# First and last norm of a hybrid trunk: a weight cast moved back, a turned tile order, paired stores

## The chip, the cores and the metric

The kernel runs on one core of one Trainium2 chip. Its time is the device time of one execution in microseconds (us), and a kernel is given by the median of several runs. Five engines work side by side, each through its own queue in order: TensorE (PE in the profile, with its weight loads as PEld), VectorE (DVE), ScalarE (ACT), GpSimd (POOL) and SyncE (SP), which issues transfers. ScalarE has a queue for transfers as well (ACTq).

## The reference

One layer of a hybrid trunk on x of 2048 tokens by 1024 features, all in float32:

```python
def rmsnorm(x, w):
    y = xf * lax.rsqrt(jnp.mean(xf * xf, axis=-1, keepdims=True) + EPS)
    return (y * w.astype(jnp.float32)).astype(x.dtype)

h = rmsnorm(x, norm_mix_w)
proj = jnp.einsum("btd,dc->btc", h, w_in)
u_b, u_c, u_h, z, xbc, dt_raw = jnp.split(proj, SPLITS, axis=-1)
y_a = short_conv_mixer(u_b, u_c, u_h, short_conv_w)
y_b = ssd_mixer(z, xbc, dt_raw, ...)
x = x + jnp.einsum("btc,cd->btd", concatenate([y_a, y_b]), w_out)
h = rmsnorm(x, norm_mlp_w)
hid = jnp.square(jax.nn.relu(jnp.einsum("btd,df->btf", h, w_up)))
x = x + jnp.einsum("btf,fd->btd", hid, w_down)
return rmsnorm(x, final_norm_w)
```

The change touches the first line (the norm ahead of the input projection, for the first 512 tokens) and the last two (the end of the down projection and the final norm, for the second 1024 tokens).

## The kernel before, in words

Features lie on the 128 partitions and tokens along the free axis: x is eight tiles of 128 features, in blocks of 512 tokens. A float32 product is made of three matmuls: each operand is split into a high part, cast by ScalarE (`whi` for weights, `uh` for data), and a low part, which VectorE subtracts (`wlo`, `ul`); the products high-high, high-low and low-high are added in PSUM. Most of the kernel multiplies by a scheme of seven products in place of eight, which is not touched here.

**The start** (`first_block`, L476 to L578). TensorE first runs 36 matmuls on a constant, `warm(on, 36)`, which nobody reads. SyncE issues, in this order: the first token rows (`tokens`), the first quarter of x, the table `cv` with norm weights and other constants (62 KB: 124 floats, 496 bytes, on each partition), three weight tiles of 512 KB (`load_w`, columns 24, 25, 26 of the input projection), and the rest of x. ScalarE squares the token rows and adds them up; square root and reciprocal give one factor for each token, with the token on the partition. To bring these factors to the free axis, VectorE multiplies the identity by them (`diag`) and TensorE multiplies ones by `diag` into the PSUM bank `prb`: each row of `prb` then holds the factors of the tokens. This is the spread. It is done in two halves of 256 columns.

Then a list written out by hand sets the order of ScalarE and VectorE. The helper `line` (its function `on`, L466 in the profile) puts each instruction behind the one before on its engine. `scale(k)` multiplies block k of x by norm weight and `prb` on VectorE and casts it on ScalarE (in two halves for k = 0), and for k above 3 it also squares a row of the next tokens on ScalarE. `lower(k)` makes the low part `ul` on VectorE. `high(i, j)` casts half j (four of the eight feature blocks) of weight tile i on ScalarE, `low(i, j)` makes its low part on VectorE. TensorE's order is fixed too, in `group`: for the first block of x it runs the high-high product of column tile 0, then its low weight, then column tile 1, then column tile 2, then the low weight of tile 1; the low weight of tile 2 comes in the next block. `low(0, 0)` stands behind `scale(0)`, and `high(0, 1)` behind `high(0, 0)`.

**The tail** (`rest`, L1196 to L1249, and `norm_out`, L1251 to L1272). After the last chain of seven products, three quarters of the down projection's outputs of the second 1024 tokens miss some terms: column pair d = 1 three blocks of features, d = 2 two, d = 3 one (`REST`, L1330). They are added by plain products, for 512 tokens first and then for two times 256. Each pair gives two tiles, d and d + 4; a tile takes 18, 12 or 6 matmuls (`mm3`) in a half of 256 tokens. VectorE adds each to what is there (L1240, the eviction), ScalarE squares it (L1217), VectorE adds the square to a running sum (L1219), except for the last tiles, whose squares are held apart. `reduce` (L129, L133 in the profile) sums over the features by matmuls with one column of ones into `pst`; `root` takes the square root on ScalarE (L149), the reciprocal on VectorE (L150) and builds the diagonal (L152); `spread` (L176) runs the spread into `prb` (L178) and copies it to SBUF on ScalarE (L181). VectorE then multiplies tiles by norm weight and `prb` (L1266). GpSimd's tiles (`slow`) don't read `prb`: they are multiplied by the norm weight on ScalarE beforehand (L1257) and by the copy on GpSimd (L1264). Each of the eight tiles is stored by a transfer of its own (L1270), in the last half four by SyncE and four by ScalarE's queue. A norm's steps are a generator: `step()` runs the next piece between the tiles of the next column block, and the framework's scheduler then sets the order on each engine.

Of the kernel before, what the change touches and what calls it, by code (L numbers as in the profile page):

```python
# [16 lines left out]
P = 128  # L17
# [22 lines left out]
def trunk(ctx: ExitStack, tc: tile.TileContext, x, x_tok, w_in, w_dt, w_out, w_up, w_down, cvec, hrow, out):  # L40
# [30 lines left out]
    cv = const.tile([P, NCV + 4], F32, name="cv")  # L71
    ident = const.tile([P, P], F32, name="ident")
# [9 lines left out]
    eps = cv[:, NCV : NCV + 1]  # L82
    nc.vector.memset(eps, EPS)
    nc.scalar.activation(cv[:, NCV + 1 : NCV + 2], eps, AF.Sqrt)
# [38 lines left out]
    class Rstd:  # L123
# [5 lines left out]
        def reduce(self, *accs):  # L129
            pst = psum("tp", "pst", 2)  # L130
            for i, acc in enumerate(accs):
                for c in range(self.n):
                    nc.tensor.matmul(  # L133
                        pst[:, c : c + 1],
                        acc[:, c * P : (c + 1) * P],
                        ones[:, 0:1],
                        start=(i + c == 0),
                        stop=(i == len(accs) - 1),
                        skip_group_check=True,
                    )  # L140
            self.sums = pst[:, 0 : self.n]
# [34 lines left out]
        def spread(self, rb=None):  # L176
            prb = self.ps = psum("tp", "prb", 2)[:, 0 : self.w]
            nc.tensor.matmul(prb, ones, self.diag, start=True, stop=True)  # L178
            if rb is None:
                rb = self.pool.tile([P, TB], F32, tag="rstd", name="rstd", bufs=1)[:, 0 : self.w]  # L180
            nc.scalar.copy(rb, prb)  # L181
            return rb
# [229 lines left out]
    class Proj(Seven):  # L412
# [63 lines left out]
        def first_block(self, fs):  # L476
# [4 lines left out]
            self.warm(on, 36)  # L481
# [3 lines left out]
            nc.sync.dma_start(cv[:, 0:NCV], cvec)  # L485
# [17 lines left out]
            more = cv[:, NCV + 2 : NCV + 3]  # L503
# [9 lines left out]
            high(0, 1)  # L513
            diag = self.tmp("diag")
            prb = psum("tp", "prb", 2)
            for j in range(2):
                cs = slice(2 * j, 2 * j + 2)
                on(
                    nc.vector.tensor_tensor,
                    out=three(diag)[:, cs],  # L520
                    in0=ident.unsqueeze(1).to_broadcast([P, 2, P]),
                    in1=rs[:, cs].unsqueeze(2).to_broadcast([P, 2, P]),
                    op=ALU.mult,
                )
                on(nc.tensor.matmul, prb[:, half(j)], ones, diag[:, half(j)], start=True, stop=True)
# [31 lines left out]
            high(2, 0)  # L557
            low(0, 0)
            lower(0)
            scale(1)  # L560
            low(1, 0)
            low(2, 0)
            scale(2)
            lower(1)
            scale(3)
# [388 lines left out]
    class Mlp(Seven):  # L954
# [241 lines left out]
        def rest(self, ws):  # L1196
# [12 lines left out]
            for bb, t0, w in ((0, 0, TB), (1, 0, TB // 2), (1, TB // 2, TB // 2)):  # L1209
# [15 lines left out]
                for (d, fs, blocks), (whi, wlo) in ws:  # L1225
                    for i in range(2):
# [3 lines left out]
                        for _ in range(1 + final if d < 3 else 1 - final):  # L1230
                            step()
# [9 lines left out]
                        alone = (d, i) in (((2, 1), (3, 0), (3, 1)) if final else ((3, 1),))  # L1241
# [9 lines left out]
        def norm_out(self, tiles, bb, ts, st, final, *sums):  # L1251
            if not final:
                st.reduce(*sums)
            st.root()
            slow = (1, 4, 5)
# [3 lines left out]
            r = st.spread()  # L1259
            yield  # L1260
            for k in range(KD):
                o = tiles[k, bb][:, ts]
                if k in slow:
                    nc.gpsimd.tensor_tensor(out=o, in0=o, in1=r, op=ALU.mult)  # L1264
                else:
                    nc.vector.scalar_tensor_tensor(  # L1266
                        out=o, in0=o, scalar=col(C_NFIN, k), in1=st.ps, op0=ALU.mult, op1=ALU.mult
                    )
                queue = nc.scalar if final and k in (1, 3, 4, 5) else nc.sync
                queue.dma_start(out[NBB + bb, :, k, ts], o)  # L1270
# [59 lines left out]
    REST = [(1, [13, 14, 15]), (2, [14, 15]), (3, [15])]  # L1330
# [459 lines left out]
def _lay_out(inputs):  # L1790
# [17 lines left out]
            vec(np.repeat(f("d_skip")[0], 64)),  # L1808
        ],
# [36 lines left out]
```

## Time and profile before

| | us |
|---|---|
| median of 3 runs | 2612.67 |
| lowest, highest | 2609.78, 2613.57 |
| the profiled execution | 2614.04 |
| its span, first to last instruction | 2612.0 |

The profile is of one execution. In the lines of a timeline, the first figure is the start in us from the span's start, the second the duration in us (of several instructions together where xN stands at the end), then engine, line, operation, output<-input, shape; in brackets stands the idle time of the engine before it and what ended that. A line of TensorE gives matmuls; ends are modelled, so that a matmul's row reaches beyond the start of the next.

### The profile page before, as it was taken

To read this page: it belongs to the slowest core of one execution; us is meant where nothing else is said; L and a number is where in the kernel's file an instruction comes from. 1 tells how busy PE (TensorE), PEld (TensorE's weight loads), DVE (VectorE), ACT (ScalarE), POOL (GpSimd) and SP (SyncE) were. 2 spreads that over 40 slices of the span, in tenths; PEclk is the share of its full clock that TensorE was granted. 3 is DMA by queue.
4 is the path that set the end of the run, shared out by engine and by line. 5 is a ranking of instruction groups with operands and counts; after the bars stand their busy time and mean duration, and the time that the engine had idled before them with its cause. 6 is when DMAs were issued, how large, how long until landed. Compare 5 with 4: busy or idle time off the path is not lost.

```text
span 2612.0 us, 33558 instructions
## 1 busy us (share of the span) xinstructions
PE 2591.7 (99%) x12067; PEld 2134.1 (82%) x12067; DVE 1936.9 (74%) x2673; ACT 1433.9 (55%) x2185; POOL 59.0 (2%) x98
## 2 busy tenths in 40 slices
PE   9999999999999999999999999999999999999998
PEld 7888888788888888888888888888888888888887
DVE  7888666677778777877767765755558877888985
ACT  7553345876667676766336555655556444444443
POOL 0000000000000000000000000000000000000001
PEclk9999999999999999999999999999999999999999
DMA  5557445555555488876665674744447644665762
GB/s 213 206 200 256 181 145 183 179 159 170 182 163 170 139 276 277 276 227 209 206 213 206 233 270 142 252 159 145 160 144 271 199 149 150 215 207 179 242 206 77
DMA packets 284375, 511.52 MB, mean 196 GB/s; under 512 B 25264, under 2 KB 140976, under 8 KB 284208
## 3 DMA queue, kind: packets, MB, share of 16 engines
q1 hardware_dynamic: 283632, 508.86, 58.2%
q8 instruction: 94, 1.54, 0.2%
q14 instruction: 73, 0.60, 0.1%
q10 hardware_dynamic: 576, 0.52, 0.1%
HBM read 345.19 MB, written 164.10 MB: 195 GB/s over the span
## 4 chain that ended last, share of the span: by engine, by line
PE 65%; issue 25%; DMA 4%; DVE 3%; ACT 2%; SPq 0%; POOL 0%; POOLq 0%; DVEq 0%; ACTq 0%
PE px L271 10%; PE px L273 9%; PE px L272 9%; PE py L271 5%; PE py L272 5%; PE py L273 5%; PE pm L114 3%; PE pm L116 3%; PE pm L115 3%; PE pw L271 2%; PE pw L272 2%; PE pw L273 2%; DMA dec<-rd_d 2%; PE pm L466 1%; PE yd L1466 1%
## 5 line engine op out<-in xcount | busy, mean ns | idle before, releaser
L271 PE MATMUL px<-uh,whi 128*128 128x512 f32 x1672 | 655.4, 392 | 3.5 <-DVE acc L1157 2.2
L272 PE MATMUL px<-ul,whi 128*128 128x512 f32 x1672 | 651.0, 389 | 0.0
L273 PE MATMUL px<-uh,wlo 128*128 128x512 f32 x1672 | 651.0, 389 | 0.0
L271 PEld LDWEIGHTS px<-uh,whi 128*128 128x128 f32 x1672 | 313.9, 188 | 75.0 <-DVE acc L1157 5.9
L106 DVE TENSOR_TENSOR wlo<-wraw,whi 128x1024 fp32r<-128x1024 f32 (+2 forms) x224 | 226.7, 1012 | 193.3 <-ACT whi L105 193.1
L273 PEld LDWEIGHTS px<-uh,wlo 128*128 128x128 f32 x1672 | 313.9, 188 | 66.0 <-issue 0.2
L272 PEld LDWEIGHTS px<-ul,whi 128*128 128x128 f32 x1672 | 314.0, 188 | 63.7
L105 ACT CAST whi<-wraw 128x1024 fp32r<-128x1024 f32 (+2 forms) x224 | 197.9, 883 | 272.6 <-PE px L272 188.7
L105 ACT CAST whi<-s 128x1024 fp32r<-128x1024 f32 (+1 forms) x206 | 215.3, 1045 | 231.2 <-PE py L272 97.7
L271 PE MATMUL py<-uh,whi 128*128 128x512 f32 x836 | 326.7, 391 | 0.0
L272 PE MATMUL py<-ul,whi 128*128 128x512 f32 x836 | 325.4, 389 | 0.0
L273 PE MATMUL py<-uh,wlo 128*128 128x512 f32 x836 | 325.4, 389 | 0.0
L106 DVE TENSOR_TENSOR wlo<-s,whi 128x1024 fp32r<-128x1024 f32 (+1 forms) x206 | 250.4, 1216 | 76.8 <-ACT whi L105 75.5
L114 PE MATMUL pm<-uh,whi 128*128 128x512 f32 (+1 forms) x584 | 226.6, 388 | 0.0
L116 PE MATMUL pm<-uh,wlo 128*128 128x512 f32 (+1 forms) x584 | 223.2, 382 | 0.0
L115 PE MATMUL pm<-ul,whi 128*128 128x512 f32 (+1 forms) x584 | 222.9, 382 | 0.0
L271 PEld LDWEIGHTS py<-uh,whi 128*128 128x128 f32 x836 | 157.0, 188 | 32.9 <-issue 0.5
L273 PEld LDWEIGHTS py<-uh,wlo 128*128 128x128 f32 x836 | 157.0, 188 | 32.8
L272 PEld LDWEIGHTS py<-ul,whi 128*128 128x128 f32 x836 | 157.0, 188 | 32.2
L325 ACT CAST uh<-rh 128x1024 fp32r<-128x1024 f32 (+1 forms) x128 | 120.2, 944 | 98.0 <-PE py L273 61.7
L271 PE MATMUL pw<-uh,whi 128*128 128x512 f32 x418 | 163.2, 391 | 0.0
L273 PE MATMUL pw<-uh,wlo 128*128 128x512 f32 x418 | 162.8, 390 | 0.0
(250 smaller groups left out, 3840.3 us busy)
## 6 DMA issues: line engine op xcount, KB each, us to landing
hid_d<-e SPq DMA_DIRECT2D x96, 512.0 KB, 4.3
rh<-hid_d SPq DMA_DIRECT2D x96, 512.0 KB, 4.5
wraw<-w_in SPq DMA_DIRECT2D x67, 512.0 KB, 4.0
wraw<-w_up SPq DMA_DIRECT2D x62, 512.0 KB, 4.3
wraw<-w_down SPq DMA_DIRECT2D x100, 256.0 KB, 3.8
dec<-rd_d SPq DMA_DIRECT2D x32, 512.0 KB, 5.3
wraw<-w_out SPq DMA_DIRECT2D x32, 512.0 KB, 5.0
x_d<-xt SPq DMA_DIRECT2D x64, 256.0 KB, 3.6
```

Of the source, the lines that this page charges most:

```text
L105: nc.scalar.copy(hi, raw)
L106: eng.tensor_tensor(out=lo, in0=raw, in1=hi.bitcast(F32), op=ALU.subtract)
L114: nc.tensor.matmul(out, whi, hi, start=(k == 0), stop=False)
L115: nc.tensor.matmul(out, whi, lo, start=False, stop=False)
L116: nc.tensor.matmul(out, wlo, hi, start=False, stop=(k == nk - 1))
L271: nc.tensor.matmul(p, hi, h[0], start=bool(first and k == 0), stop=False, **kw)
L272: nc.tensor.matmul(p, hi, h[1], start=False, stop=False, **kw)
L273: nc.tensor.matmul(p, lo, h[0], start=False, stop=(k == len(g) - 1), **kw)
L325: nc.scalar.copy(p[i][0], t)
L466: last[engine] = make(*args, **kw).ins
L1466: nc.tensor.matmul(yd[(i % 2) * 64 : (i % 2) * 64 + 64, (i // 2) * L : (i // 2 + 1) * L], byhead(t["xdt"])[:, i, :], t["dec"][:, i, :], st ...
```

## The change

At the start: the table `cv` gets four columns of zeros on the host and is loaded as rows of 512 bytes; the constants that stood in its last columns move to a tile `small`. One warm-up matmul fewer. The diagonal is built by one instruction and spread by one matmul of 512 columns. `high(0, 1)` moves from behind `high(0, 0)` to behind `lower(1)`; `high(2, 0)` moves from ahead of `low(0, 0)` to behind `scale(1)`.

In the tail: `REST` runs d = 3, 2, 1, so the small tiles come first. In the last half two squares are held apart, not three. Behind the last sum matmul four matmuls of 512 columns on a constant run in a bank of their own. The last half's spread is run twice, into two banks: VectorE reads one, ScalarE copies the other. In the last half GpSimd multiplies two tiles (2 and 3) and VectorE six; before it were three and five; in the other blocks GpSimd's three are 2, 3 and 6 in place of 1, 4 and 5. In the last half tiles are multiplied into pair buffers, in the order 0, 1, 4, 5, 2, 3, 6, 7, and stored two at a time: pairs (0, 1) and (6, 7) by SyncE, (4, 5) and (2, 3) by ScalarE's queue.

```diff
+    small = const.tile([P, 4], F32, name="small")
-    eps = cv[:, NCV : NCV + 1]
+    eps = small[:, 0:1]
-    nc.scalar.activation(cv[:, NCV + 1 : NCV + 2], eps, AF.Sqrt)
+    nc.scalar.activation(small[:, 1:2], eps, AF.Sqrt)
...
-            self.sums = pst[:, 0 : self.n]
+            self.sums, self.reduced = pst[:, 0 : self.n], mm.ins
...
-        def spread(self, rb=None):
+        def spread(self, rb=None, apart=False):
             prb = self.ps = psum("tp", "prb", 2)[:, 0 : self.w]
             nc.tensor.matmul(prb, ones, self.diag, start=True, stop=True)
+            if apart:
+                prb = psum("mw", "prb")[:, 0 : self.w]
+                nc.tensor.matmul(prb, ones, self.diag, start=True, stop=True)
...
-            self.warm(on, 36)
+            self.warm(on, 35)
-            nc.sync.dma_start(cv[:, 0:NCV], cvec)
+            nc.sync.dma_start(cv, cvec)
-            more = cv[:, NCV + 2 : NCV + 3]
+            more = small[:, 2:3]
...
             high(0, 0)
-            high(0, 1)
             diag = self.tmp("diag")
             prb = psum("tp", "prb", 2)
-            for j in range(2):
-                cs = slice(2 * j, 2 * j + 2)
-                on(
-                    nc.vector.tensor_tensor,
-                    out=three(diag)[:, cs],
-                    in0=ident.unsqueeze(1).to_broadcast([P, 2, P]),
-                    in1=rs[:, cs].unsqueeze(2).to_broadcast([P, 2, P]),
-                    op=ALU.mult,
-                )
-                on(nc.tensor.matmul, prb[:, half(j)], ones, diag[:, half(j)], start=True, stop=True)
+            on(
+                nc.vector.tensor_tensor,
+                out=three(diag),
+                in0=ident.unsqueeze(1).to_broadcast([P, NC, P]),
+                in1=rs.unsqueeze(2).to_broadcast([P, NC, P]),
+                op=ALU.mult,
+            )
+            on(nc.tensor.matmul, prb, ones, diag, start=True, stop=True)
...
             scale(0)
             high(1, 0)
-            high(2, 0)
             low(0, 0)
             lower(0)
             scale(1)
+            high(2, 0)
             low(1, 0)
             low(2, 0)
             scale(2)
             lower(1)
+            high(0, 1)
             scale(3)
...
-                        for _ in range(1 + final if d < 3 else 1 - final):
+                        for _ in range(1 + final if d > 1 else 1 - final):
                             step()
-                        alone = (d, i) in (((2, 1), (3, 0), (3, 1)) if final else ((3, 1),))
+                        alone = d == 1 and i >= 1 - final
...
             if not final:
                 st.reduce(*sums)
+            else:
+                p = psum("mw", "pw")
+                with behind(st.reduced):
+                    for _ in range(4):
+                        nc.tensor.matmul(
+                            p, ones_r, ones_r.unsqueeze(1).to_broadcast([P, 4, P]), start=True, stop=True
+                        )
             st.root()
-            slow = (1, 4, 5)
+            slow = (2, 3) if final else (2, 3, 6)
...
-            r = st.spread()
+            r = st.spread(apart=final)
             yield
-            for k in range(KD):
-                o = tiles[k, bb][:, ts]
+            pair = None
+            for k in (0, 1, 4, 5, 2, 3, 6, 7) if final else range(KD):
+                o = to = tiles[k, bb][:, ts]
+                if final:
+                    if k % 2 == 0:
+                        pair = self.raw("fo")[:, :, 0 : st.w]
+                    to = pair[:, k % 2]
                 if k in slow:
-                    nc.gpsimd.tensor_tensor(out=o, in0=o, in1=r, op=ALU.mult)
+                    nc.gpsimd.tensor_tensor(out=to, in0=o, in1=r, op=ALU.mult)
                 else:
                     nc.vector.scalar_tensor_tensor(
-                        out=o, in0=o, scalar=col(C_NFIN, k), in1=st.ps, op0=ALU.mult, op1=ALU.mult
+                        out=to, in0=o, scalar=col(C_NFIN, k), in1=st.ps, op0=ALU.mult, op1=ALU.mult
                     )
-                queue = nc.scalar if final and k in (1, 3, 4, 5) else nc.sync
-                queue.dma_start(out[NBB + bb, :, k, ts], o)
+                if not final:
+                    nc.sync.dma_start(out[NBB + bb, :, k, ts], o)
+                elif k % 2:
+                    queue = nc.scalar if k in (3, 5) else nc.sync
+                    queue.dma_start(out[NBB + bb, :, k - 1 : k + 1, ts], pair)
...
-    REST = [(1, [13, 14, 15]), (2, [14, 15]), (3, [15])]
+    REST = [(3, [15]), (2, [14, 15]), (1, [13, 14, 15])]
...
+            np.zeros((P, 4), np.float32),
```

More of the change, by code (lines that the diff above doesn't have):

```diff
@@ L132, in reduce @@
                 for c in range(self.n):
-                    nc.tensor.matmul(
+                    mm = nc.tensor.matmul(
                         pst[:, c : c + 1],
```

## The prediction

> **What bounds the kernel now.** I read the page first, then the timeline of each engine over the first 33 us and the last 30 us, since the diff touches nothing between, and last the waits and the DMA landings of those stretches.
>
> ```profile
> PE 2591.7 (99%) x12067; PEld 2134.1 (82%) x12067; DVE 1936.9 (74%) x2673; ACT 1433.9 (55%) x2185; POOL 59.0 (2%) x98
> ```
>
> TensorE (PE) is busy for 99% of the span, so the end moves only with what TensorE waits for at the start, with what stands in its queue, and with the tail after its last matmul. The two changed places are of that kind. At the start, first TensorE, then ScalarE (ACT):
>
> ```profile
> 11.29 1.02 PE L466 MATMUL prb<-diag,ones_r 128*128 128x256 f32 x4
> ...
> 14.28 0.50 PE L466 MATMUL pm<-uh,whi 128*128 128x512 f32 x1 [1.27 <-ACT uh L466]
> ...
> 15.72 0.50 PE L466 MATMUL pm<-uh,whi 128*128 128x512 f32 x1
> ...
> 24.86 0.96 PE L466 MATMUL pm<-ul,whi 128*128 128x512 f32 x3 [0.33 <-DVE ul L466]
> ```
>
> ```profile
> 12.48 1.14 ACT L466 CAST whi<-wraw 128x512 fp32r<-128x512 f32 x2 [2.39 <-DMA wraw<-w_in]
> 13.52 0.71 ACT L466 CAST uh<-x 128x256 fp32r<-128x256 f32 x2
> 14.13 0.62 ACT L466 CAST whi<-wraw 128x512 fp32r<-128x512 f32 x1
> 15.04 0.62 ACT L466 CAST whi<-wraw 128x512 fp32r<-128x512 f32 x1 [0.29 <-DMA wraw<-w_in]
> 15.64 0.62 ACT L466 CAST uh<-x 128x512 fp32r<-128x512 f32 x1
> ```
>
> The first real matmul starts at 14.28, after 1.27 us without work, released by the cast `uh` on ScalarE. Ahead of that cast stand two weight casts (12.48, two in 1.14 us), and the first of them waited 2.39 us for the first weight to land. So the landing of the weight at about 12.45, then 0.52 us for each cast ahead, then 0.71 us for the two `uh` halves set 14.28. VectorE (DVE) in the same stretch:
>
> ```profile
> 10.40 0.76 DVE L466 TENSOR_TENSOR diag<-ident,rs 128x256 f32<-128x256 f32 x2
> 12.35 0.87 DVE L466 SCALAR_TENSOR_TENSOR x<-x,cv,prb 128x256 f32<-128x256 f32 x2 [1.19 <-PE prb L466]
> 13.14 0.68 DVE L466 TENSOR_TENSOR wlo<-wraw,whi 128x512 fp32r<-128x512 f32 x1
> 14.26 0.69 DVE L466 TENSOR_TENSOR ul<-x,uh 128x512 fp32r<-128x512 f32 x1 [0.43 <-ACT uh L466]
> 14.87 0.74 DVE L466 SCALAR_TENSOR_TENSOR x<-x,cv,prb 128x512 f32<-128x512 f32 x1
> 15.53 1.28 DVE L466 TENSOR_TENSOR wlo<-wraw,whi 128x512 fp32r<-128x512 f32 x2
> ```
>
> In these rows VectorE has one gap, 0.43 us for `uh`. It makes all low parts, and the last wait of TensorE in its rows is at 24.86, for VectorE's `ul` of the fifth block. So this start is bound first by ScalarE and then by VectorE's queue: a gain at 14.28 counts only if it is still there at 24.86.
>
> The tail, TensorE, ScalarE, VectorE, GpSimd (POOL), then DMA issues with KB and median us to landing:
>
> ```profile
> 2596.09 0.60 PE L178 MATMUL prb<-diag,ones_r 128*128 128x256 f32 x2
> ...
> 2601.19 0.28 PE L116 MATMUL pm<-uh,wlo 128*128 128x256 f32 x1
> 2601.31 0.50 PE L133 MATMUL pst<-ones_r,facc 128*128 128x1 f32 x4
> 2601.95 1.50 PE L133 MATMUL pst<-ones_r,sq 128*128 128x1 f32 x12
> 2604.46 0.70 PE L178 MATMUL prb<-diag,ones_r 128*128 128x256 f32 x2 [1.01 <-DVE diag L152]
> ```
>
> ```profile
> 2596.78 0.38 ACT L181 COPY rstd<-prb 128x256 f32<-128x256 f32 x1 [0.28 <-PE prb L178]
> ...
> 2601.48 1.08 ACT L1217 ACTIVATE sq<-acc 128x256 f32<-128x256 f32 x3 [1.03 <-DVE acc L1240]
> 2603.48 0.26 ACT L149 ACTIVATE rs<-pst,cv 128x2 f32<-128x2 f32 x1 [0.93 <-PE pst L133]
> 2605.53 0.37 ACT L181 COPY rstd<-prb 128x256 f32<-128x256 f32 x1 [1.78 <-PE prb L178]
> ```
>
> ```profile
> 2601.03 1.08 DVE L1240 TENSOR_TENSOR acc<-pm,acc 128x256 f32<-128x256 f32 x3
> 2603.78 0.17 DVE L150 RECIPROCAL rs<-rs 128x2 f32<-128x2 f32 x1 [1.67 <-ACT rs L149]
> 2603.98 0.42 DVE L152 TENSOR_TENSOR diag<-ident,rs 128x256 f32<-128x256 f32 x1
> 2605.93 2.05 DVE L1266 SCALAR_TENSOR_TENSOR acc<-acc,cv,prb 128x256 f32<-128x256 f32 x5 [1.53 <-ACT rstd L181]
> ```
>
> ```profile
> 2605.98 2.09 POOL L1264 TENSOR_TENSOR acc<-acc,rstd 128x256 f32<-128x256 f32 x3 [6.60 <-ACT rstd L181]
> ```
>
> ```profile
> L1270 ACTq DMA_DIRECT2D out<-acc x4: 407/440/955, 2606.7 to 2608.8; - x4
> ```
>
> ```profile
> out<-acc SPq DMA_DIRECT2D x8, 256.0 KB, 2.4
> ...
> out<-acc ACTq DMA_DIRECT2D x4, 128.0 KB, 2.3
> ```
>
> The last product matmul starts at 2601.19 and the span ends at 2612.0: 10.8 us in which nothing but the last norm runs. It is a chain: three evictions in a row (2601.03, 1.08 us), three squares (to 2602.56), twelve sum matmuls (to 2603.45), root 2603.48, diagonal to 2604.40, spread 2604.46, copy 2605.53 to 2605.90, five VectorE products (to 2607.98) beside three of GpSimd (to 2608.07), then stores. ScalarE issues four of them one after the other (its queue's row: shortest, median and longest issue in ns, then first and last start); the last starts at 2608.8 and lands 2.3 us later, at 2611.1.
>
> **The change, part by part.** All times are of the profiled execution.
>
> *Table in 512-byte rows, constants in a tile of their own.* The table's transfer stands ahead of the three weight loads in SyncE's queue. The weight that releases 12.48 and the one that releases 15.04 lie two transfers of 512 KB apart, 2.56 us, so 64 KB are worth 0.16 us. The table still moves its bytes, so the gain lies between 0 and 0.16 us; I take 0.05, nearer to nothing.
>
> *One warm-up matmul fewer, diagonal whole.* Two halves of the diagonal end at 11.16 (10.40 and 0.76), and the spread's four matmuls run from 11.29 to 12.31; VectorE starts only when all four are done. One diagonal and one spread of the same columns end some 0.1 us sooner at best, 0.1 us later at worst (the first spread no longer overlaps the second diagonal). Cost nothing: ScalarE starts at 12.48 whatever the spread does, and VectorE's third piece, `wlo` at 13.14, needs that cast. Without that cover it would be 0.1 us.
>
> *Second half of the first weight cast later, third weight's cast behind the second block.* ScalarE's order becomes: first weight cast 12.48, `uh` at 13.00 to 13.71, so TensorE starts at 13.76, 0.52 us sooner. VectorE's `ul` starts at 13.75 (its queue is free at 13.75 also), and the product of the second block at 14.36 in place of 14.87. Its result is ready at 14.36 + 0.74 = 15.10, the second `uh` cast runs from 15.13, and only behind it, 0.52 us later at 15.65, the third weight's cast, which ran at 15.04 before, when its data landed. It ends at 15.65 + 0.62 = 16.27. Two waits stand behind it. TensorE's matmul of the third column, 15.72 before, starts at 16.32, 0.60 us later, and all first-block matmuls behind it wait. VectorE's second `wlo` of the pair at 15.53 started at 15.53 + 0.60 = 16.13; it now starts at 16.30, and every VectorE piece behind it moves by 0.17 us. The half cast that was taken from the front goes in further back on ScalarE, between two casts that wait for VectorE anyway. The wait that ends last is the `ul` at 24.86, which comes from VectorE's queue: 0.17 us later. So the front gain of 0.52 us is used up by the new wait. Ends: -0.52 us (all of it survives) and +0.60 us (TensorE never catches up the third column); I take +0.17, by VectorE's rows, because TensorE had 0.33 us of slack there. With the table: +0.12 us at the start.
>
> *Tiles in turned order.* The same matmuls, squares and additions run; the small tiles (six matmuls at a half) come first and the tile with eighteen last. Now three tiles end within 1.5 us of TensorE time and VectorE bunches their evictions; with eighteen matmuls between, one eviction is left. Last matmul end 2601.47, eviction 0.42 us (the diagonal's row at 2603.98 has the same engine and columns), square 0.36 us (a third of 1.08) to 0.42, of which I take the upper, four sum matmuls 0.50 us (the row at 2601.31), with 0.03 to 0.05 us for each hand-off: 2601.50, 2601.95, 2602.42, 2602.92. The root starts at 2602.95, not 2603.48: -0.53 us. The sums of the other tiles (eight matmuls, 1.0 us) run on TensorE meanwhile. The loading order of the weights turns with it; the last of them is now needed later than the first tile, so I cost that at nothing, covered by the matmuls of three blocks.
>
> *Four full-width fill matmuls behind the sums.* From the root to the diagonal's end 0.92 us pass (2603.48 to 2604.40), in which TensorE idles 1.01 us before the spread. Four fills of 512 columns at 0.24 us (twice the step of 0.12 us from 2601.19 to 2601.31, which has half the columns) take about 0.96 us behind the sums, 2602.9 to 2603.9; the diagonal ends at 2603.87. So they end between 0.1 us before it and 0.2 us behind. What they can buy is the spread's time: at 2596.09, on a busy TensorE, the copy starts 0.69 us after the spread; at 2604.46, after idling, 1.07 us. The effect lies between +0.2 us (they only delay) and -0.38. I take -0.38, because the 2596.09 spread is the same instruction on a busy engine.
>
> ```profile
> 2605.00:2606.00 1.00, 0.15 (x1) 0.00 (x0) 0.07 (x1) 0.37 (x1) 0.02 (x1) 1.00 0.00 0
> ```
>
> The granted clock in the microsecond behind that spread is 1.00 (third figure from the end of the row, ahead of DMA share and GB/s). By the Trainium skill, TensorE: Matmul & The Clock Gate, section on the HAM clock gate, the clock halves only after an idle window of about 3.4 us; by that rule fills across 1 us buy nothing and can only stand in the way. The row agrees with it, and the 1.07 us do not; by the rule the whole sum would be about -0.9 us, an estimate.
>
> *Two spreads, one per reader.* VectorE waited 1.53 us, until ScalarE's copy from the same bank was over (2605.90). With a bank each it starts behind the first spread: 2602.95 + 0.92 + 0.06 + 0.69 = 2604.62, so 2604.65 in place of 2605.93. The second spread puts the copy 0.3 to 0.5 us behind: 2604.9 to 2605.1, and GpSimd at about 2605.4. GpSimd has two products left, 0.70 us each (a third of 2.09): done at 2606.8. VectorE has six at 0.41: done at 2607.1.
>
> *Stores of two tiles.* Four issues in place of eight, two per queue. SyncE's first at 2605.55; ScalarE's first at 2606.35 and its second behind it. ScalarE's longest issue took 0.955 us, and with three of 0.41 to 0.44 between 2606.7 and 2608.8 I take it to be its first, so the second starts near 2607.3; SyncE's last at 2607.15. A 256 KB store lands 2.4 us after issue: 2609.7 and 2609.6, where 2611.1 stood. Tail: -1.4 us, between -0.8 (spread as slow as now, fills 0.2 us in the way) and -1.6 (square 0.36 us, ScalarE's first issue as short as the others, so that SyncE's last store decides).
>
> Sum: +0.12 - 1.4 = -1.3 us. The profiled execution took 2614.04 us (span 2612.0 and 2.0 around it) and would take 2612.7; it lies 1.4 us above the median of 2612.67, which goes to 2611.4. About 0.2%, 5.2 us, is what a measurement of this kernel can tell from no change, and its three runs alone spread from 2609.78 to 2613.57.
>
> **Rivals.**
> *The joints lose their cover (slower).* At each of the two joints between column blocks the norm's chain (eviction 0.42, square 0.42, sums 0.50, root to diagonal 0.92, spread 0.69: 3.0 us) is hidden behind product matmuls of the next block. These now begin with two tiles of six. If TensorE's queue takes the spread ahead of the longer tiles, twelve matmuls at 0.12 us cover 1.4 us and 1.6 us is lost per joint; if it takes none ahead, 3.0 us, twice, 6.0 us: 2612.67 + 6.0 - 1.3 = 2617.4. It decides once fewer than 25 matmuls stand ahead of the spread. Against it: the spread at 2596.09 has no idle time before it, and four tiles, 36 matmuls, 4.3 us, fit into four banks.
> *The fills buy nothing.* Tail -1.0: 2611.8. For it speaks the granted clock.
> *The start keeps its 0.52 us.* The third column would have to be caught up: 2612.67 - 0.57 - 1.4 = 2610.7. Against it: VectorE's wait at 16.30.
> *The stores decide (the change doesn't do what it says).* If the larger stores share the DMA engines so that the last lands as late as eight small ones, only the issues saved on ScalarE count, 0.3 us: 2612.4.
>
> **How the numbers follow.** Forecast 0.50, fills 0.22, start kept 0.12, stores 0.12, joints 0.04. All but the last lie within 0.2% of 2612.67; the joints' dearest case is at its edge. Same 0.95, slower 0.02, faster 0.03: these last are left for a run-to-run spread and a middle part that settles otherwise. The range takes in the cases from 2610.7 to 2612.4 and 2 us either way for the spread of the runs: 2608.7 to 2614.4.
>
> **What would show it.** At the start: first matmul near 13.76, the third weight's cast behind the second `uh` at about 15.65, a wait of VectorE ahead of its `wlo` near 16.30, and the fifth block's `ul` matmuls at about 25.0. In the tail, from the last product matmul: root 1.75 us behind its start (2.3 before), VectorE's first product 3.45 us behind (4.7 before), the span's end 9.4 us behind (10.8 before). It is wrong if TensorE shows new idle time at the joints, if the spread still takes 1.07 us, or if the first matmul's gain is still there behind 25 us.

## The result and the profile after

| | us |
|---|---|
| before, median of 4 runs | 2611.23 (2609.53 to 2613.57) |
| after, median of 4 runs | 2667.99 (2666.63 to 2673.64) |
| ratio, 95% interval | 1.0216 (1.0204 to 1.0228) |
| profiled execution after, its span | 2668.3, 2666.4 |

The kernel became 2.2% slower. The two edited places lie at the two ends of the span; 54.4 us were added (2666.4 against 2612.0), and nearly all of them came in between, where no instruction was edited. The page's first part, after:

```profile
PE 2652.4 (99%) x12066; PEld 2137.6 (80%) x12066; DVE 1941.5 (73%) x2674; ACT 1432.6 (54%) x2184; POOL 56.1 (2%) x97
```

The row counts one matmul fewer than before, and TensorE (PE) is busy 60.7 us longer (2652.4 against 2591.7). Its time without work fell from 20.3 to 14.0 us. So nothing is waited for: the matmuls themselves go slower. VectorE, ScalarE and the weight loads (PEld) take what they took, within 5 us. A stretch of 100 us far from both edits, from the table of stretches of before and then of after (busy time and, in brackets, instructions of PE, PEld, DVE, ACT, POOL; then granted clock, DMA share, GB/s):

```profile
200.00:300.00 100.00, 100.00 (x443) 82.79 (x442) 79.80 (x103) 37.92 (x47) 8.39 (x11) 1.00 0.65 239
```

```profile
200.00:300.00 100.00, 100.00 (x430) 80.64 (x429) 77.05 (x99) 38.39 (x48) 6.03 (x11) 1.00 0.65 238
```

TensorE is never idle in either, the granted clock is 1.00 in both, the DMA load is the same, and 430 matmuls go through in place of 443. The largest group of matmuls in the pages, before and after (count, busy us, mean ns of one):

```profile
L271 PE MATMUL px<-uh,whi 128*128 128x512 f32 x1672 | 655.4, 392 | 3.5 <-DVE acc L1157 2.2
```

```profile
L275 PE MATMUL px<-uh,whi 128*128 128x512 f32 x1672 | 665.1, 398 | 1.8 <-ACT pw L283 1.4
```

6 ns more for each. A row's duration overlaps the next matmul; the honest measure is the step from one start to the next. From one product matmul of 512 columns to the next such there are 10,535 steps; over those up to 300 ns (10,401 before, 10,414 after; longer ones hold waits) the mean is 227.1 ns before and 233.3 ns after. All 10,535 together, waits included, take 61.9 us more; TensorE's other steps take 7.4 us less, and the difference is the 54.4 us.

At the start, after, in TensorE's, ScalarE's and VectorE's timelines:

```profile
1.12 10.50 PE L470 MATMUL pw<-ones_r 128*128 128x512 f32 x35 [1.12 <-DVE small L84]
11.49 1.12 PE L470 MATMUL prb<-diag,ones_r 128*128 128x512 f32 x2
...
14.02 0.50 PE L470 MATMUL pm<-uh,whi 128*128 128x512 f32 x1 [0.71 <-ACT uh L470]
...
16.61 0.50 PE L470 MATMUL pm<-uh,whi 128*128 128x512 f32 x1 [1.10 <-ACT whi L470]
...
25.34 0.94 PE L470 MATMUL pm<-ul,whi 128*128 128x512 f32 x3
```

```profile
12.12 0.62 ACT L470 CAST whi<-wraw 128x512 fp32r<-128x512 f32 x1 [1.70 <-DMA wraw<-w_in]
13.17 0.80 ACT L470 CAST uh<-x 128x256 fp32r<-128x256 f32 x2 [0.43 <-DVE x L470]
...
15.95 0.61 ACT L470 CAST whi<-wraw 128x512 fp32r<-128x512 f32 x1
```

```profile
16.59 0.69 DVE L470 TENSOR_TENSOR wlo<-wraw,whi 128x512 fp32r<-128x512 f32 x1 [0.60 <-ACT whi L470]
```

The first product matmul comes 0.26 us sooner than before, the third column 0.89 us later (16.61 against 15.72) behind a new wait of 1.10 us, and the fifth block's `ul` matmuls 0.48 us later. They have no wait ahead of them now: TensorE reaches them just when VectorE has made the `ul` (24.58 and 0.69 us).

The tail, after, in the timelines of TensorE (from the last product matmul), ScalarE, VectorE, GpSimd and the queues:

```profile
2655.69 0.28 PE L117 MATMUL pm<-uh,wlo 128*128 128x256 f32 x1
...
2657.40 1.17 PE L1260 MATMUL pw<-ones_r 128*128 128x512 f32 x4
2658.56 0.70 PE L179 MATMUL prb<-diag,ones_r 128*128 128x256 f32 x2
```

```profile
2657.58 0.26 ACT L150 ACTIVATE rs<-pst,small 128x2 f32<-128x2 f32 x1 [0.69 <-PE pst L134]
...
2661.66 1.05 ACTq L1287 DMA_DIRECT2D out<-fo  x2
```

```profile
2659.29 2.44 DVE L1280 SCALAR_TENSOR_TENSOR fo<-acc,cv,prb 128x256 f32<-128x256 f32 x6 [0.79 <-PE prb L179]
```

```profile
2660.23 1.40 POOL L1278 TENSOR_TENSOR fo<-acc,rstd 128x256 f32<-128x256 f32 x2 [7.36 <-ACT rstd L185]
```

From the start of the last product matmul the root comes after 1.89 us (2.29 before), VectorE's first product after 3.60 us (4.74 before), the span's end after 10.7 us (10.8 before). The chain gained 1.1 us and the end 0.1 us: the stores gave it back. ScalarE's queue issues its first store at 2661.66, when GpSimd's pair is done (2660.23 + 1.40), though VectorE's second pair was ready at about 2660.92, after four products of 0.41 us. So three of the four stores leave within 0.6 us, and the DMA engines are full behind them (DMA share: the figure ahead of GB/s); then the stores with KB and median us to landing:

```profile
2663.00:2664.00 1.00, 0.00 (x0) 0.00 (x0) 0.00 (x0) 0.00 (x0) 0.00 (x0) 0.50 1.01 342
2664.00:2665.00 1.00, 0.00 (x0) 0.00 (x0) 0.00 (x0) 0.00 (x0) 0.00 (x0) 0.50 1.00 330
```

```profile
out<-fo SPq DMA_DIRECT2D x2, 256.0 KB, 2.4
out<-fo ACTq DMA_DIRECT2D x2, 256.0 KB, 3.1
```

The first store, alone, lands 2.1 us after its issue, the last one 3.2 us after it.

### The profile page after: what moved, and what is told of

Its sections match the earlier page's. It is cut to its first block, busy times and chain, and to the rows that moved or that the text cites. A ratio compares the mean times of both kernels' runs of the same rounds, so it can differ in the third digit from the quotient of the medians.

```text
span 2666.4 us, 33562 instructions
## 1 busy us (share of the span) xinstructions
PE 2652.4 (99%) x12066; PEld 2137.6 (80%) x12066; DVE 1941.5 (73%) x2674; ACT 1432.6 (54%) x2184; POOL 56.1 (2%) x97
## 4 chain that ended last, share of the span: by engine, by line
PE 97%; DMA 1%; ACT 1%; DVE 1%; issue 0%; SPq 0%; DVEq 0%; ACTq 0%
PE px L275 14%; PE px L276 14%; PE px L277 14%; PE py L275 7%; PE py L276 7%; PE py L277 7%; PE pm L115 5%; PE pm L116 5%; PE pm L117 5%; PE pw L275 4%; PE pw L276 4%; PE pw L277 4%; PE pm L470 2%; PE yd L1483 1%; PE yo L1480 1%; DMA dec<-rd_d 1%
## 5 line engine op out<-in xcount | busy, mean ns | idle before, releaser
L275 PE MATMUL px<-uh,whi 128*128 128x512 f32 x1672 | 665.1, 398 | 1.8 <-ACT pw L283 1.4
L276 PE MATMUL px<-ul,whi 128*128 128x512 f32 x1672 | 662.0, 396 | 0.0
L277 PE MATMUL px<-uh,wlo 128*128 128x512 f32 x1672 | 661.9, 396 | 0.0
L107 DVE TENSOR_TENSOR wlo<-wraw,whi 128x1024 fp32r<-128x1024 f32 (+1 forms) x224 | 226.9, 1013 | 211.3 <-ACT whi L106 211.0
L106 ACT CAST whi<-wraw 128x1024 fp32r<-128x1024 f32 (+1 forms) x224 | 197.3, 881 | 296.3 <-PE px L276 209.3
L275 PE MATMUL py<-uh,whi 128*128 128x512 f32 x836 | 332.2, 397 | 0.0
L276 PE MATMUL py<-ul,whi 128*128 128x512 f32 x836 | 331.0, 396 | 0.0
L277 PE MATMUL py<-uh,wlo 128*128 128x512 f32 x836 | 330.9, 396 | 0.0
L276 PE MATMUL pw<-ul,whi 128*128 128x512 f32 x418 | 165.6, 396 | 0.0
```

What stands on the lines that cost most here:

```text
L106: nc.scalar.copy(hi, raw)
L107: eng.tensor_tensor(out=lo, in0=raw, in1=hi.bitcast(F32), op=ALU.subtract)
L275: nc.tensor.matmul(p, hi, h[0], start=bool(first and k == 0), stop=False, **kw)
L276: nc.tensor.matmul(p, hi, h[1], start=False, stop=False, **kw)
L277: nc.tensor.matmul(p, lo, h[0], start=False, stop=(k == len(g) - 1), **kw)
```

## The experiments

What the diff does to every matmul is in none of its edited instructions. The program's own list of tile addresses (the trace does not show them) gave the suspect: the new tile `small`, four floats, takes 32 bytes of every partition, and all that is allocated behind it on that side of SBUF lies 32 bytes higher. Among it are the weight tiles: the first `whi` begins at byte 15776 in place of 15744. The moving data (`uh`, `ul`) is allocated from the other side and stays at 114560. The first theory was that the weight tile's own address matters (15744 is a multiple of 128), the rivals that the edits themselves or other tiles do it. Where no ratio is given below, a time is of one run; the kernel before took 2612.07 to 2621.44 us on the same chips.

**The whole change without a shift.**

```diff
-    small = const.tile([P, 4], F32, name="small")
...
+    hbs = const.tile([P, 64], F32, name="hb")
+    hb, small = hbs[:, 0:32], hbs[:, 32:36]
...
-    hb = const.tile([P, 64], F32, name="hb")[:, 0:32]
```

> The whole change, but the constants lie in four unused columns of an existing tile, so that no SBUF address moves against the kernel before. Theory A (address: the new 16-byte tile takes 32 bytes and pushes the weight tiles 32 bytes on, which costs some 6 ns at each matmul of 512 columns): the matmul step is back at 227 ns and the time at the kernel before less 1 to 2 us, 2609 to 2611. Theory B (the start: one warm-up matmul fewer and an earlier first matmul leave TensorE at a slower pace for the whole run): step 233 ns, 2666 to 2668. Theory C (queue orders that the scheduler changed, or the turned tail): between 2655 and 2668.

Measured: 2616.93 us against 2614.57 of before on the same chip, ratio 1.0006 (0.9996 to 1.0015), step 227.1 ns. Everything that the change computes and moves is in this kernel; the loss is gone. The 1 to 2 us that it was to be faster than before are not there.

**The kernel before with nothing but a shift of 32 bytes.**

```diff
     cv = const.tile([P, NCV + 4], F32, name="cv")
+    pad = const.tile([P, 4], F32, name="pad")
+    nc.gpsimd.memset(pad, 0.0)
```

> The kernel before with nothing but an unused tile of 16 bytes behind the table, cleared once by GpSimd: every tile behind it on that side moves by 32 bytes. Theory A: step 233 ns and some 2667 us. Theories B and C: step 227 ns, 2609 to 2614.

Measured: 2668.45 us, step 233.3 ns, and in the table of stretches:

```profile
200.00:300.00 100.00, 100.00 (x431) 80.49 (x430) 76.93 (x98) 38.38 (x48) 7.25 (x11) 1.00 0.67 239
```

A tile that nobody reads makes the whole loss.

**Which tiles, and which grid.** Two kernels: the change with `small` 64 bytes wide, and the kernel before with a pad behind the weight tiles, so that only the staging tiles behind them move.

```diff
-    small = const.tile([P, 4], F32, name="small")
+    small = const.tile([P, 16], F32, name="small")
```

> The whole change with the new tile at 64 bytes in place of 16: everything behind it moves by 64 bytes. Theory A with a 64-byte grid: step 227 ns, about 2610 us. Theory A with a coarser grid (128 bytes and more): slower than 2640. Theories B and C: 2667 whatever the width.

```diff
+    pad = keep.tile([P, 4], F32, name="pad")
+    nc.gpsimd.memset(pad, 0.0)
```

> The kernel before with the unused 16-byte tile behind the weight tiles: only the tiles of the stages (sums, staging, accumulators) move by 32 bytes, the weight tiles and the split data don't. Theory A, if it is the weights that TensorE reads: 227 ns and 2609 to 2614 us. Theory A, if it is the writes and reads of the other engines that get in TensorE's way: 230 to 233 ns, 2640 to 2667 us.

Measured: 2667.53 us and 233.3 ns with 64 bytes; 2620.69 us and 227.1 ns with the pad behind. So it is the weight tiles, and a shift of 64 bytes is as bad as one of 32.

**The weights' address, or their distance from the moving data.** The kernel before with the weight tiles 128 bytes lower, with the moving data 64 bytes lower, and with both 64 bytes lower:

```diff
-    hb = const.tile([P, 64], F32, name="hb")[:, 0:32]
+    hb = const.tile([P, 32], F32, name="hb")
```

> The kernel before with one edit: the rope/bias table's tile hb is allocated with the 32 columns that are used in place of 64, so every tile behind it on that side, the weight tiles among them, lies 128 bytes lower (first weight tile at byte 15616 in place of 15744). Everything else is the same, the computation whole. Theory A, a grid of 128 bytes for the weight tiles: 15616 and 15744 are both multiples of 128, so the step from one 512-column product matmul to the next stays at 227.1 ns and the time at 2610 to 2621 us. Rival G, a coarser grid (the old place, 384 above a multiple of 512, is the one good place, or places 256 apart are): the step goes to about 233 ns and the time to about 2667 us. Rival H, 15744 was itself only half as good as a multiple of 256: the step falls below 226 ns and the time by 10 us or more.

```diff
-    edge = ctx.enter_context(tc.tile_pool(name="edge", bufs=1, side="right")).tile([P, 24], F32, name="edge")
+    edge = ctx.enter_context(tc.tile_pool(name="edge", bufs=1, side="right")).tile([P, 40], F32, name="edge")
```

> The kernel before with one edit: the small tile at the edge of the other side of SBUF is 64 bytes wider, so that the moving data (uh and ul) and everything else on that side lie 64 bytes lower (114496 in place of 114560), while the weight tiles stay at 15744. Theory A, the weight tile's own address decides: step 227.1 ns, time 2610 to 2621 us. Rival R, the distance between weight tile and moving data decides: the distance is 64 bytes off, as in the experiment that moved the weights by 64 bytes, so the step goes to about 233 ns and the time to 2667 us. Rival M, the moving data has a grid of its own as well: the step also leaves 227.1 ns (this run alone cannot tell R from M, the next one does).

```diff
-    edge = ctx.enter_context(tc.tile_pool(name="edge", bufs=1, side="right")).tile([P, 24], F32, name="edge")
+    edge = ctx.enter_context(tc.tile_pool(name="edge", bufs=1, side="right")).tile([P, 40], F32, name="edge")
...
-    hb = const.tile([P, 64], F32, name="hb")[:, 0:32]
+    hb = const.tile([P, 48], F32, name="hb")[:, 0:32]
```

> The kernel before with two edits: hb is 48 columns wide in place of 64, which puts the weight tiles 64 bytes lower (15680, which is 64 above a multiple of 128), and the edge tile is 64 bytes wider, which puts the moving data 64 bytes lower too, so that their distance is what it was. Theory A, the weight tile's own address: step about 233 ns, time about 2667 us. Rival R, the distance: step 227.1 ns, time 2610 to 2621 us. Rival M, both grids add up: a step above 234 ns, time above 2680 us.

The same stretch in the three, in this order:

```profile
200.00:300.00 100.00, 100.00 (x432) 81.11 (x431) 77.45 (x98) 38.41 (x48) 6.03 (x11) 1.00 0.67 240
```

```profile
200.00:300.00 100.00, 100.00 (x431) 80.66 (x430) 77.11 (x98) 38.40 (x48) 6.03 (x11) 1.00 0.66 239
```

```profile
200.00:300.00 100.00, 100.00 (x443) 82.86 (x442) 79.56 (x103) 37.91 (x47) 8.37 (x11) 1.00 0.65 240
```

2660.9, 2665.56 and 2618.9 us; steps 232.5, 233.3 and 227.1 ns. The first theory falls: 128 bytes lower the weights are on its grid and slow, and 64 bytes lower, off it, they are fast as long as the moving data goes with them. What decides is the distance between the two, and moving the data alone costs the same as moving the weights.

**The distance by itself.** A small program of matmuls alone; its core:

```diff
+            lhs = wt[:, (w + 512 * (k % 2)) // 4 :][:, 0:P]
...
+                last[0] = nc.tensor.matmul(
+                    p, lhs, mv[:, at // 4 : at // 4 + cols], start=(k == 0), stop=(k == n - 1)
+                ).ins
```

> A small program in place of the whole computation: none of the reference is computed, the output is filled with one constant tile. TensorE alone runs groups of 100 matmuls of 128x128 fp32r weights, taken in turn from two places 512 bytes apart, with 512 columns of moving data, into one PSUM bank; from group to group only the byte distance between the place of the moving data and that of the weights changes (0, 16, 32, 64 and so on to 1024, modulo 512 when both tiles begin on the same phase), then four groups in which weights and moving data are shifted together, and five with 256 columns. No other engine works meanwhile. Theory R, the distance between weights and moving data decides: groups at distance 0, 512 and 1024 and all groups shifted together take 100 x 227 ns = 22.7 us, groups at 32, 64 and at 384 (128 below 512) about 23.3 us; whether 256 belongs to the good or to the bad ones is open. With 256 columns the whole kernel showed the other sign (119.6 ns at distance 0, 117.0 to 118.4 off it), so 12.0 us at 0 and 11.7 to 11.8 at 32 and 64. Rival P, pressure by the other engines is needed (VectorE and ScalarE reading and writing SBUF at the same time): then all groups of 512 columns take the same time here, between 21.3 and 22.8 us. Rival S, the three-way pattern of high and low tiles is what matters and not the distance as such: the same, all groups alike.

TensorE's timeline; the name of the bank gives the distance in bytes ("both": weights and data shifted together, "half": 256 columns):

```profile
19.83 23.00 PE L56 MATMUL at0b<-mv,wt 128*128 128x512 f32 x100 [0.79 <-DVE res L59]
...
67.83 23.60 PE L56 MATMUL at32b<-mv,wt 128*128 128x512 f32 x100 [0.79 <-DVE res L59]
92.21 23.16 PE L56 MATMUL at64b<-mv,wt 128*128 128x512 f32 x100 [0.78 <-DVE res L59]
...
140.54 23.59 PE L56 MATMUL at128b<-mv,wt 128*128 128x512 f32 x100 [0.79 <-DVE res L59]
...
189.29 22.98 PE L56 MATMUL at256b<-mv,wt 128*128 128x512 f32 x100 [0.78 <-DVE res L59]
...
237.01 23.51 PE L56 MATMUL at384b<-mv,wt 128*128 128x512 f32 x100 [0.78 <-DVE res L59]
...
310.07 22.99 PE L56 MATMUL at512b<-mv,wt 128*128 128x512 f32 x100 [0.78 <-DVE res L59]
...
381.38 22.96 PE L56 MATMUL both32b<-mv,wt 128*128 128x512 f32 x100 [0.78 <-DVE res L59]
...
476.38 12.26 PE L56 MATMUL half0b<-mv,wt 128*128 128x256 f32 x100 [0.79 <-DVE res L59]
489.15 11.94 PE L56 MATMUL half32b<-mv,wt 128*128 128x256 f32 x100 [0.52 <-DVE res L59]
```

23.0 us for 100 at distances 0, 256, 512, 768 and 1024, whatever the addresses; 23.2 to 23.6 us at the ten others tried. No other engine works during a group, so neither their pressure nor the pattern of high and low parts is needed. The size fits as well: weights moved up by 32 or 64 bytes make the distance (data minus weights) 224 or 192 modulo 256, and at 192, 448 and 480 the small program loses 6 ns for each matmul (23.59 to 23.60 us). The loss is not the same everywhere off 0: it is smallest at 64 and 320 (23.16 and 23.17 us). With 256 columns the sign turns: 12.26 us at 0 and 256, 11.94 at 32. In the whole kernel, too: the last column block's products of 256 columns stepped by 119.6 ns before and 118.4 after.

**A distance of 256 bytes in the whole kernel.**

```diff
-    hb = const.tile([P, 64], F32, name="hb")[:, 0:32]
+    hb = keep.tile([P, 64], F32, name="hb")[:, 0:32]
```

> The kernel before with one edit: the hb tile, 256 bytes in each partition, is allocated behind the weight tiles in place of ahead of them, so the weight tiles lie 256 bytes lower (15488 in place of 15744) and the moving data stays. The computation is whole. Theory R with a period of 256 bytes, as the small program had it (23.0 us for 100 matmuls at distances 0, 256, 512, 768 and 1024, up to 23.6 us at all others): step 227.1 ns, 443 matmuls per 100 us, time 2610 to 2621 us. Rival, a period of 512 bytes in the whole kernel, or an address of the weights that counts by itself: step above 232 ns, time above 2655 us.

Measured: 2617.09 us, step 227.1 ns, 443 matmuls in the stretch. The period is 256 bytes here too.

**The two edited places, mended.** With the shift out of the way (the constants in `hb`'s free columns, as in the first experiment), what the start and the tail lose can be undone: the third weight's cast at its old place, and ScalarE's queue with pairs that VectorE makes.

```diff
             high(1, 0)
+            high(2, 0)
             low(0, 0)
...
             scale(1)
-            high(2, 0)
...
-                    queue = nc.scalar if k in (3, 5) else nc.sync
+                    queue = nc.scalar if k in (5, 7) else nc.sync
```

> The whole change with its small constants in unused columns of the hb tile (no tile moves), and two edits more: the third weight's first half is cast where it was before the change, ahead of the first low parts, and ScalarE's queue stores the last two VectorE pairs (tiles 4,5 and 6,7) while SyncE stores the first pair and GpSimd's pair. Theory: weight tiles at their old addresses, so the step is 227.1 ns. Start: no wait of 1.09 us of TensorE ahead of the third column, and the fifth block's ul matmuls at about 24.9 (25.3 after the change, 26.9 in the run without the shift). Tail: the last store is issued 6.1 us behind the last product matmul's start and the span ends about 10.0 us behind it, in place of 10.7. Both together 1 to 2 us less than the run without the shift, ratio to the kernel before about 0.9995, inside what runs of this kernel spread. Rival: the four stores share the DMA engines, so that the order of issues does not matter: end 10.7 behind. Rival: the start's loss is the granted clock, which falls again whatever the order: ul matmuls at 26 to 27 with a clock below 0.9 in the rows of 17 to 21 us.

Measured: 2613.63 us against 2616.18, ratio 0.9990 (0.9981 to 0.9999). TensorE's start, and in the tail TensorE's last sums and the queues:

```profile
13.91 0.50 PE L470 MATMUL pm<-uh,whi 128*128 128x512 f32 x1 [0.70 <-ACT uh L470]
...
15.31 0.50 PE L470 MATMUL pm<-uh,whi 128*128 128x512 f32 x1
...
24.53 0.96 PE L470 MATMUL pm<-ul,whi 128*128 128x512 f32 x3 [0.29 <-DVE ul L470]
...
2600.71 0.28 PE L117 MATMUL pm<-uh,wlo 128*128 128x256 f32 x1
```

```profile
2606.00 1.19 ACTq L1287 DMA_DIRECT2D out<-fo  x2
```

The wait ahead of the third column is gone, the `ul` matmuls come 0.33 us sooner than in the profile before the change. ScalarE's first store leaves 5.29 us behind the last product matmul in place of 5.97, and the span of 2610.7 ends 9.99 us behind it: 0.8 us less than before. Together that would be 1.1 us; that the runs say 2.6 us lies within their interval. Only the tail's part stands out from one execution to the next: the end comes 10.8 to 11.4 us behind the last product matmul in the profiles with the old tail, but the `ul` matmuls at 24.37 to 25.82 us in those with the old start.

**The diagonal in halves again**, on top of that, with 36 warm-up matmuls:

> The mended version (constants in unused columns, third weight's cast at its old place, stores re-ordered) with the diagonal of the first norm in two halves again and one warm-up matmul more, as before the change. Theory: with one weight cast less ahead of it, ScalarE's uh cast no longer hides the spread, it waits for VectorE's first product (0.38 us in the mended version); the whole diagonal puts that product 0.2 us later (12.55 against 12.35 before), so with halves the wait is about 0.2 us, TensorE's first real matmul starts near 13.7 in place of 13.91, and VectorE's queue and the fifth block's ul matmuls are 0.2 us earlier (24.3 in place of 24.53). Time 0.2 us less than the mended version, which the runs cannot tell; the end of the span 10.0 us behind the last product matmul's start again. Rival: the later product came from later token rows in that execution and not from the diagonal; then the product starts at 12.5 again and nothing moves.

```diff
-            self.warm(on, 35)
+            self.warm(on, 36)
...
-            on(
-                nc.vector.tensor_tensor,
-                out=three(diag),
...
+            for j in range(2):
+                cs = slice(2 * j, 2 * j + 2)
```

Measured: 2612.19 us against 2615.55, ratio 0.9988 (0.9979 to 0.9997), the fastest version tried by its ratio, though not apart from the one before it. Its profile cannot answer its question, because the third token rows landed late in that execution:

```profile
8.11 1.06 ACT L470 ACTIVATE tok<-tok 128x1024 f32<-128x1024 f32 x1 [1.18 <-DMA tok<-x_tok]
```

That squaring began at 7.18 before the change, so the whole start is about 0.9 us late. What a whole diagonal costs by itself stays open.

## Why the prediction was wrong, step by step

**The step that failed** is its first sentence, "the diff touches nothing between", on which some 2,550 us of the span were carried over unchanged. The tile `small` was costed, with the table, at a few hundredths of a microsecond, as if a tile cost only the instructions that touch it. Its term for the matmuls in between was 0; the whole change measured +54.4 us in the profiled spans, and the unused tile alone +53.9 us (2668.45 against 2614.57). What the runs show in place of "touches nothing" is that each of some 10,400 product matmuls takes 6 ns more when the tile moves the weights against the data by 32 bytes. None of the rivals had it: all of them were about the two edited places. The page of before could not show it, since a trace gives no addresses; the diff could, because an allocation ahead of other allocations moves them.

**The table.** Its gain was taken as 0.05 us, at most 0.16. The first weight's cast began at 12.12 after, 12.22, 12.06 and 12.20 in the kernels with the change and no shift, 12.48 before: 0.26 to 0.42 us sooner. But in the six kernels built on the one before, with the old table, it began between 11.77 and 13.45. So these profiles can't tell the gain from nothing, and its size stays open.

**Warm-up and diagonal, "cost nothing".** The cover named was ScalarE's wait for the weight. That covers the first cast, but the `uh` cast behind it needs VectorE's first product, and with one weight cast less ahead ScalarE was there first and waited 0.43 us. The product came 0.30 us later (12.65 against 12.35), mostly because the spread stood in TensorE's queue until 11.49 (11.29 before): 35 warm-up matmuls took 10.50 us, 36 had taken 10.33. They start one in 0.43 us until 5.98 (until 5.13 before) and one in 0.23 us from there; in the other whole kernels that moment lies between 4.27 and 7.14 us, so the 0.85 us between these two can be chance. In the mended version the diagonal was ready at 10.98 and the spread began at 11.49 all the same, so it was TensorE's queue.

**Weight casts moved.** The front gain did not come: from the first weight's cast to the first product matmul 1.90 us passed (1.80 before, 1.28 forecast), for the reason just given. First matmul 14.02 where 13.76 was forecast, third weight's cast 15.95 for 15.65, third column 16.61 for 16.32, `wlo` 16.59 for 16.30, `ul` 25.34 for 25.0: the new wait as described, each step 0.26 to 0.34 us later than forecast, which is about the 0.30 us of the point above. The start cost 0.48 us and not 0.12. That the wait came from the moved cast is shown by the mended version, where it is gone. Counted from the first product matmul, the `ul` matmuls come after 11.32 us with the cast moved, and after 10.57 to 10.62 us in the nine kernels with this cast in its old place. That VectorE's rows alone set the end is not shown: TensorE, its 0.33 us of slack used up, came to the `ul` at the same moment.

**Turned order, fills, two spreads.** Root 1.89 us behind the last product matmul (1.75 forecast), first product 3.60 (3.45), six products in 2.44 us (0.41 each, as taken). From the spread to its reader it took 0.73 us, where 0.69 was taken and 1.07 stood before; whether the fills or the second spread did that was not tried apart.

**Stores.** The end came 10.7 us behind, not 9.4. The step took ScalarE's first store to be VectorE's pair, at 2606.35 on the old scale; the scheduler had put GpSimd's pair ahead of it on that queue. So the last store left 6.56 us behind the last product matmul, not about 6.1. The larger part of the miss is the landing: 3.2 us for that store where 2.4 was taken, with the DMA engines full. That is the mechanism of the stores' rival, and of the four rivals it came nearest for this place. Given to the queues by readiness, the stores gained 0.7 us: the last one leaves 6.08 us behind and lands 3.0 us later, so that 9.99 is still 0.6 above the forecast, by the landing.

## What to carry to other kernels

Read a diff for what it allocates as well as for what it issues: a tile put ahead of others moves them, and when every matmul gets a few ns slower with the clock granted and the waits unchanged, compare the tile addresses of the two programs. Keep the weights' and the moving data's places equal modulo 256 bytes where fp32r matmuls of 512 columns bound the kernel, and put small constants behind the large tiles or into columns that are free. A cover named for one instruction holds only for that one: follow it to the next reader, and on a queue look at what stands ahead of each store. Count on it that stores leaving together land later than one alone (3.2 against 2.1 us here).

## What the runs showed of the hardware

With fp32r weights of 128x128 and 512 columns of data, the step depended on the distance between weights and data modulo 256 bytes: 227 ns at 0 and 232 to 233 ns at the others tried in the whole kernel (128, 192 and 224). Why, and why 256 columns prefer the reverse (12.26 against 11.94 us for 100), no run here shows. By the Trainium skill, SBUF — State Buffer, section "Operand start alignment", an operand must start at a multiple of its element size, and it says that this is about legality and not speed; every placement here fulfils that, and they differ by 2%.

In the whole change without a shift, the granted clock fell at the start though TensorE's longest wait there was 1.09 us (third figure from the end):

```profile
16.00:17.00 1.00, 0.28 (x1) 0.28 (x2) 0.40 (x2) 0.67 (x2) 0.00 (x0) 0.87 1.07 430
17.00:18.00 1.00, 1.00 (x3) 0.81 (x4) 1.00 (x3) 0.00 (x0) 0.00 (x0) 0.50 0.99 393
```

It stayed at 0.50 until 20 and cost that execution about 1.5 us (`ul` matmuls at 26.86 against 25.34 after the change, where the clock stayed at 1.00 with the same wait). By the Trainium skill, TensorE: Matmul & The Clock Gate, section on the HAM clock gate, it takes an idle window of about 3.4 us; the idle time here was shorter. The clock records of the traces show more than that. After the first grant (here at 6.50 us) the clock changes only whole multiples of 3.41 us later: it fell at 16.74 and came back at 20.16. Cut into stretches of 3.41 us from that grant, the twelve profiles of whole kernels show eight falls away from the end of the span; ahead of each, TensorE was without work for 1.63 to 2.35 us of the stretch, and no stretch without a fall behind it had more than 1.57 us. Here both waits (0.70 and 1.09 us) lie in one stretch, 13.33 to 16.74. After the change the cut falls into the second wait, and the stretch from 12.83 to 16.25 holds 1.44 us without work. That fits the difference between the two executions; no run was made to test it.
